# A decoder layer: x for the sums loaded one item sooner on the weight queue, both fifth products of a group in one item, and more steps ahead of two heads' transposes

## The chip, the cores and the metric

The kernel runs on one core of a Trainium2 chip. The metric is device time in microseconds (us) of one launch, the median of several runs. Names of engines: PE is TensorE (PEld its weight loads), DVE is VectorE, ACT is ScalarE, POOL is GpSimd, SP is the SyncE, which here only issues DMAs. "L505" is line 505 of the kernel before.

## The reference

One layer on x of 512 tokens by 1024 channels, in float32. A combined projection gives the columns of three token mixers and three gates. Cut to what matters here:

```
proj = x @ w_in                       # 1024 x 10752
da:  4 heads of differential attention (two softmax maps, lambda, RMS norm, relative bias)
sb:  8 heads of stick-breaking attention (log-space breaks, strictly causal)
dil: 12 heads of dilated windows, 3 groups (window, dilation) x 4 head slots; the three
     outputs of a head slot are weighed by their softmax denominators
merged = sigmoid(g0) * (o_da @ w_branch_da) + sigmoid(g1) * (o_sb @ w_branch_sb)
       + sigmoid(g2) * (o_dil @ w_branch_dil)
x = layer_norm(alpha * x + merged @ w_out)
x = layer_norm(alpha * x + square(relu(x @ w_up)) @ w_down + sigmoid(x @ w_ple_gate) * (p @ w_ple))
```

## The kernel before

**Products.** Every large product keeps close to float32 accuracy by splitting both operands into a high and a low part: `mm3` issues three matmuls (L89 to L91), high by high, high by low, low by high. A weight chunk of 128 x 1024 is loaded into `raw`, ScalarE casts its high part to `wh` (L263), VectorE subtracts to get `wl` (L265). Six `raw` and five `wh`/`wl` buffers go round, so a cast waits until TensorE has finished with the chunk five back.

**Seven products for eight.** Some of the projections (the pairs of dilated values, the query/key groups, the gates, and later the large layers) are cut into 2 x 2 blocks and computed with seven block products instead of eight. That needs sums of weight blocks and sums of x blocks. The sums of weight blocks are made by DMAs from GpSimd that accumulate in memory (`sum_steps`, L1183), one 512 KB transfer a step. The sums of x blocks are made on chip: `load_xr` (L498) loads x again as eight tiles `xr` of 256 KB, each held back until the last weight split issued so far is done; `mixer_forms` (L682) waits five steps, then subtracts blocks on VectorE (L690, L695, L696, L700) and splits the results into the forms u7, u6, u4, u5 (L292, L293).

**Items.** The work of TensorE is a list of items, run in order by the main loop (from L2134). Per item the loop: evacuates the item before (`ev`); issues splits and loads of weights (`pump`, `fill`); adds `size * rate` of the item to a credit, each whole unit of which issues one sum step; runs one step of everything that is in progress beside the items; and issues the item's matmuls. Items of single projections and of da_v give one more step halfway through their matmuls.

The order of items around the change: single projections, four items of da_v, then 14 items of a pair of values (`value_pair`, L531, at `pair_at`), then two groups of eight items (`group_items`, L354), four single projections, a third group, four single projections, then the first branch product and the gates. A group computes the projections of two query/key pairs (j = 0 and 1) with seven products of 256 columns. Its items are: second product for both j; first product for both; seventh and sixth for j = 0, for j = 1; fifth for j = 0, for j = 1 (`of_five`, L436); third and fourth for j = 0, for j = 1. Each is three matmuls by four blocks: a product of one j is 12 matmuls.

**Steps.** Each attention head is a generator that does its next piece at each step; at most eight accumulator banks' worth of heads are in progress, in a fixed order (stick-breaking first, then dilated heads 0, 1, 2, then the differential ones). A dilated head (`dil_head`, L1948) does: first logits (L1965) with their maxima (L1968) and exponentials (L1974); the other logits (L1981, L1989) and exponentials (L1996), and r, the statistics spread for a matmul (L1999, L2002); two steps later the exchange of statistics between partitions (px, L2007 and L2009) and the scaling of the weights (L2031, L2035); then, once all values are there, two transposes into two banks (L2055) with copies pt, one step later two more (L2064), and one step later the output products (L2073, L2078). Their values come through memory: `keep` (L519) stores the projected values on the weight queue, `values_of` (L523) reads them back per head as dl_vh (L528), also on that queue. Head 0 reads them one step after all values are stored, then waits two more steps ahead of its transposes; heads 1 and 2 wait none there; head 3 one.

**Order on the engines.** Items and steps give each instruction its place in the program's text; the order on each engine is then planned when the program is built, by dependences, that order and the planner's own estimates of time, so an instruction can be put ahead of one that comes earlier in the text. On the chip each engine, and each DMA queue's issuer, runs its list strictly in order. Waits for buffers are part of it: a load waits until the tile's former use has ended.

The step count and places that the change touches are numbers in the main loop: `forms_at` is the item at which `mixer_forms` begins, `DA_TABS` the item at which the bias tables of the differential heads are loaded (they are turned six items later).

Of the kernel before, what the change touches and what calls it, by code (L numbers as in the profile page):

```python
# [57 lines left out]
def trunk(tc, a, out):  # L58
    nc = tc.nc
    es = ExitStack()  # L60
    with es:
# [223 lines left out]
        items = []  # L285
# [14 lines left out]
        xt = a["xT"]  # L300
# [53 lines left out]
        def group_items(gi, pairs):  # L354
# [21 lines left out]
            def add(ps, need, free, run, ev, bank):  # L376
                for p in ps:
                    at = {5: 0, 6: 1, 7: 2, 3: 3}.get(p)
                    cs[p] = [chunk(w[{1: 0, 2: 1, 4: 3}[p]] if at is None else qsum[gi][at], 1024)]
                item([c for p in free for c in cs[p]], lambda b: run(), lambda b: ev(),  # L380
                     need=[c for p in need for c in cs[p]], bank=bank)
                items[-1]["rate"] = 0.6

            def put(j, i, h, ps, s=None):

# [47 lines left out]
                    nc.scalar.copy(b["s"][:, HB], b["x"][:, HC])  # L433
                add(() if j else (7, 6), (7, 6), (7, 6) if j else (), run, ev, lambda: both[j]["x"])

            def of_five(j):  # L436
                def run():
                    prod(j, 5, HB, False, False)

                def ev():  # L440
                    put(j, 1, 1, both[j]["x"][:, HB], both[j]["s"][:, HB])
                add(() if j else (5,), (5,), (5,) if j else (), run, ev, lambda: both[j]["x"])

            def of_three_four(j):
                def run():
# [9 lines left out]

            of_two()
            of_one()
            for f in (of_seven_six, of_five, of_three_four):
                for j in range(2):
                    f(j)  # L460

        def first_item():

# [34 lines left out]
        def load_xr():  # L498

            r = {}  # L500
            for h in range(2):
                for th in range(2):
                    for kp in range(2):
                        t = slot("xr")
                        i = nc.gpsimd.dma_start(t.rearrange("p (k t) -> p k t", k=2),  # L505
                                                xt[:, 4 * h + 2 * kp:4 * h + 2 * kp + 2, 256 * th:256 * th + 256])
                        tc.add_manual_dep(getattr(i, "ins", i), lows[-1].name, mybir.DependencyInfo(
                            mybir.DependencyClass.Sync, mybir.DependencyReason.DATA), reason="not ahead of time")
                        r[h, th, kp] = t
            return [[r[h, th, kp] for kp in range(2)] for h in range(2) for th in range(2)]  # L510
# [171 lines left out]
        def mixer_forms():  # L682

            r11, r12, r21, r22 = load_xr()
            for _ in range(5):
                yield

            with tc.issue_after(st["low"]):
                for kp in range(2):
                    nc.vector.tensor_sub(r22[kp], r22[kp], r12[kp])  # L690
            form(xf, 7, r22)
            yield
            for kp in range(2):
                with tc.issue_after(st["low"]):
                    nc.vector.tensor_sub(r12[kp], r11[kp], r12[kp])  # L695
                nc.vector.scalar_tensor_tensor(r11[kp], r22[kp], -1.0, r11[kp], op0=OP.mult, op1=OP.subtract)  # L696
            form(xf, 6, r11)
            yield
            for kp in range(2):
                nc.vector.scalar_tensor_tensor(r21[kp], r11[kp], -1.0, r21[kp], op0=OP.mult, op1=OP.subtract)  # L700
            form(xf, 4, r21)
            yield
            form(xf, 5, r12)
            yield
# [1243 lines left out]
        def dil_head(hd):  # L1948
# [91 lines left out]
            if hd == 0:  # L2040
                yield
                values = values_of(hd)
            for _ in range({0: 2, 3: 1}.get(hd, 0)):
                yield

            src0 = {}
# [77 lines left out]
                except StopIteration:  # L2124
                    pending.remove(g)

        DA_TABS = pair_at[0] + 22
        sum_steps_ = sum_steps()
        credit = 0.0
        forms_at = pair_at[0] - 5  # L2130
        freed = 0
        prev = None
        for n, it in enumerate(items):
# [196 lines left out]
```

## Time and profile before

| | us |
|---|---|
| median of 3 runs | 1054.31 (1051.61 to 1055.39) |
| the profiled execution's own time | 1055.07 |
| its span, first to last instruction | 1053.4 |
| TensorE busy | 1029.4 |
| VectorE busy | 778.7 |
| ScalarE busy | 615.6 |
| GpSimd busy | 198.3 |
| mean granted TensorE clock | 0.989 |

The span starts and ends with the core's first and last instruction; the execution's own time is 1.67 us longer. Times in the views count from the start of the span. In a row of a timeline stand the start, the duration (of a merged run of instructions, the whole run's), the engine, line and operation, output and inputs, and in brackets the idle time just before and what ended it. In a row of windows stand the window, its length, the busy time of TensorE, its weight loads, VectorE, ScalarE and GpSimd with their instruction counts, the granted clock, the busy share of the DMA engines and GB/s. A row of waits has the total, the number of times and the longest.

### The profile page before, as it was taken

The page shows a single profiled execution, that of the slowest core. Times are in us where ns is not written, and L with a number is a line of the kernel's source. Part 1 is how long each engine was busy: PE and PEld are TensorE (multiplying, and loading weights), DVE is VectorE, ACT ScalarE, POOL GpSimd, SP SyncE. Part 2 cuts the span into 40 slices and gives each one's busy share as a digit, 9 for nine tenths or more (in the row PEclk, how much of TensorE's full clock was granted, in tenths as well). Part 3 has the DMA queues.
Part 4 walks back from the last instruction along what each step waited for, and adds up shares of the span by engine and source line. Part 5 has one row for each costly group of instructions (what it writes and reads, how often), then busy time and mean ns, then how long its engine had stood idle before and what let it go on. Part 6 is the DMA issues. An engine that isn't in the chain of part 4 may idle for free.

```text
span 1053.4 us, 15640 instructions
## 1 busy us (share of the span) xinstructions
PE 1029.4 (98%) x5650; PEld 889.5 (84%) x5650; DVE 778.7 (74%) x1387; ACT 615.6 (58%) x1057; POOL 198.3 (19%) x299
## 2 busy tenths in 40 slices
PE   9999999899889999999999999999999999999996
PEld 7888888778779898888888888888999899899885
DVE  6888567577645777667879885888678777777975
ACT  7575466365334566565775753685656566566651
POOL 0314421211102122121301122121212112111001
PEclk9999999899989999999999999999999999999998
DMA  8999997559968969787899999379999999998622
GB/s 305 290 277 290 252 305 258 160 135 270 298 223 257 305 227 276 168 233 215 240 299 258 298 294 306 76 198 325 344 328 323 325 326 331 306 319 270 214 76 80
DMA packets 83629, 270.74 MB, mean 257 GB/s; under 512 B 9720, under 2 KB 16648, under 8 KB 83552
## 3 DMA queue, kind: packets, MB, share of 16 engines
q0 software_dynamic: 35984, 128.79, 48.6%
q1 hardware_dynamic: 46992, 140.04, 36.4%
q8 instruction: 44, 0.72, 0.3%
q10 hardware_dynamic: 576, 0.92, 0.2%
q14 instruction: 33, 0.27, 0.1%
HBM read 262.35 MB, written 112.22 MB: 356 GB/s over the span
## 4 chain that ended last, share of the span: by engine, by line
PE 67%; DVE 2%; ACT 0%; issue 0%; DVEq 0%
PE mm L89 6%; PE mm L90 6%; PE mm L91 6%; PE at L1401 4%; PE at L1402 4%; PE at L1403 4%; PE at L721 3%; PE at L723 3%; PE at L722 3%; PE at L89 2%; PE at L90 2%; PE at L91 2%; PE at L1014 1%; PE at L1013 1%; PE at L1012 1%; PE at L1140 1%
## 5 line engine op out<-in xcount | busy, mean ns | idle before, releaser
L265 DVE TENSOR_TENSOR wl<-raw,wh 128x1024 fp32r<-128x1024 f32 x268 | 323.2, 1214 | 130.6 <-ACT wh L263 129.1
L263 ACT CAST wh<-raw 128x1024 fp32r<-128x1024 f32 x268 | 278.0, 1043 | 218.8 <-PE mm L90 112.7
L89 PE MATMUL mm<-xhT,wh 128*128 128x512 f32 (+1 forms) x254 | 95.5, 376 | 0.0
L91 PE MATMUL mm<-xhT,wl 128*128 128x512 f32 (+1 forms) x254 | 94.2, 371 | 0.0
L90 PE MATMUL mm<-xlT,wh 128*128 128x512 f32 (+1 forms) x254 | 94.2, 371 | 0.0
L1401 PE MATMUL at<-wh,hh 128*128 128x512 f32 x188 | 73.7, 392 | 0.0
L1402 PE MATMUL at<-wl,hh 128*128 128x512 f32 x188 | 73.7, 392 | 0.0
L1403 PE MATMUL at<-wh,hl 128*128 128x512 f32 x188 | 73.1, 389 | 0.0
L89 PE MATMUL mm<-x1hT,wh 128*128 128x256 f32 x256 | 72.8, 284 | 0.0
L90 PE MATMUL mm<-x1lT,wh 128*128 128x256 f32 x256 | 72.4, 283 | 0.0
L91 PE MATMUL mm<-x1hT,wl 128*128 128x256 f32 x256 | 72.4, 283 | 0.0
L91 PEld LDWEIGHTS mm<-xhT,wl 128*128 128x128 f32 x254 | 47.8, 188 | 8.2
L89 PEld LDWEIGHTS mm<-xhT,wh 128*128 128x128 f32 x254 | 47.9, 189 | 7.7 <-PE mm L590 0.2
L90 PEld LDWEIGHTS mm<-xlT,wh 128*128 128x128 f32 x254 | 47.9, 189 | 7.5
L89 PEld LDWEIGHTS mm<-x1hT,wh 128*128 128x128 f32 x256 | 48.9, 191 | 1.9
L90 PEld LDWEIGHTS mm<-x1lT,wh 128*128 128x128 f32 x256 | 48.9, 191 | 1.5
L91 PEld LDWEIGHTS mm<-x1hT,wl 128*128 128x128 f32 x256 | 48.9, 191 | 0.0
L1218 POOL DMA_DIRECT2D usum<-in_wu_dram x32 | 29.8, 942 | 93.9 <-DMA usum<-usum 30.7
L1218 POOL DMA_DIRECT2D dsum<-in_wd_dram x28 | 24.4, 870 | 117.6 <-DVE wl L265 38.1
L1403 PEld LDWEIGHTS at<-wh,hl 128*128 128x128 f32 x188 | 35.3, 188 | 7.7
L1401 PEld LDWEIGHTS at<-wh,hh 128*128 128x128 f32 x188 | 35.5, 189 | 6.2
L1402 PEld LDWEIGHTS at<-wl,hh 128*128 128x128 f32 x188 | 35.5, 189 | 5.7
(672 smaller groups left out, 2863.7 us busy)
## 6 DMA issues: line engine op xcount, KB each, us to landing
usum<-in_wu_dram POOLq DMA_DIRECT2D x48, 512.0 KB, 8.9
dsum<-in_wd_dram POOLq DMA_DIRECT2D x42, 512.0 KB, 8.7
raw<-usum SPq DMA_DIRECT2D x32, 512.0 KB, 8.3
raw<-dsum SPq DMA_DIRECT2D x28, 512.0 KB, 8.4
raw<-in_wt_dram SPq DMA_DIRECT2D x26, 512.0 KB, 6.8
raw<-in_wd_dram SPq DMA_DIRECT2D x25, 512.0 KB, 6.2
raw<-in_wu_dram SPq DMA_DIRECT2D x24, 512.0 KB, 8.1
raw<-in_wv_dram SPq DMA_DIRECT2D x18, 512.0 KB, 6.9
```

Of the source, the lines that this page charges most:

```text
L89: nc.tensor.matmul(ps, wh, xh, start=start, stop=False, skip_group_check=True)
L90: nc.tensor.matmul(ps, wh, xl, start=False, stop=False, skip_group_check=True)
L91: nc.tensor.matmul(ps, wl, xh, start=False, stop=stop, skip_group_check=True)
L263: i = nc.scalar.copy(h, raw)
L265: i = nc.vector.tensor_sub(lo, raw, h.bitcast(F32))
L721: nc.tensor.matmul(ps, h[:, q], c["h"][:, n], start=go, stop=False, skip_group_check=True)
L722: nc.tensor.matmul(ps, h[:, q], c["l"][:, n], start=False, stop=False, skip_group_check=True)
L723: nc.tensor.matmul(ps, lo[:, q], c["h"][:, n], start=False, stop=end, skip_group_check=True)
L1218: i = nc.gpsimd.dma_start(o, i, accum_op=OP.add, max_dma_last_dim=4096)
L1401: nc.tensor.matmul(ps, h[:, q], c["h"][:, s], start=go, stop=False, skip_group_check=True)
L1402: nc.tensor.matmul(ps, h[:, q], c["l"][:, s], start=False, stop=False, skip_group_check=True)
L1403: nc.tensor.matmul(ps, lo[:, q], c["h"][:, s], start=False, stop=end, skip_group_check=True)
```

## The change

In each group both fifth products become one item, so a group has seven items instead of eight, and the credit of a group's item goes from 0.6 to 0.85. The eight loads of xr are issued by SP instead of GpSimd; `mixer_forms` begins one item sooner and waits six steps instead of five. Head 0 waits four steps instead of two ahead of its transposes, and head 1 one instead of none. The bias tables are loaded two item numbers sooner.

```
-                items[-1]["rate"] = 0.6
+                items[-1]["rate"] = 0.85
...
-            def of_five(j):
+            def of_five():
                 def run():
-                    prod(j, 5, HB, False, False)
+                    for j in range(2):
+                        prod(j, 5, HB, False, False)
+                        if not j:
+                            put(0, 1, 1, both[0]["x"][:, HB], both[0]["s"][:, HB])
 
                 def ev():
-                    put(j, 1, 1, both[j]["x"][:, HB], both[j]["s"][:, HB])
-                add(() if j else (5,), (5,), (5,) if j else (), run, ev, lambda: both[j]["x"])
+                    put(1, 1, 1, both[1]["x"][:, HB], both[1]["s"][:, HB])
+                add((5,), (5,), (5,), run, ev, lambda: None)
...
-            for f in (of_seven_six, of_five, of_three_four):
-                for j in range(2):
-                    f(j)
+            for j in range(2):
+                of_seven_six(j)
+            of_five()
+            for j in range(2):
+                of_three_four(j)
...
-                        i = nc.gpsimd.dma_start(t.rearrange("p (k t) -> p k t", k=2),
-                                                xt[:, 4 * h + 2 * kp:4 * h + 2 * kp + 2, 256 * th:256 * th + 256])
+                        i = nc.sync.dma_start(t.rearrange("p (k t) -> p k t", k=2),
+                                              xt[:, 4 * h + 2 * kp:4 * h + 2 * kp + 2, 256 * th:256 * th + 256])
...
             r11, r12, r21, r22 = load_xr()
-            for _ in range(5):
+            for _ in range(6):
                 yield
...
-            for _ in range({0: 2, 3: 1}.get(hd, 0)):
+            for _ in range({0: 4, 1: 1, 3: 1}.get(hd, 0)):
                 yield
...
-        DA_TABS = pair_at[0] + 22
+        DA_TABS = pair_at[0] + 20
         sum_steps_ = sum_steps()
         credit = 0.0
-        forms_at = pair_at[0] - 5
+        forms_at = pair_at[0] - 6
```

## The prediction

> **What bounds the kernel now.** I read the page first, then TensorE's waits over the whole span, then the windows around the slices in which its clock digit falls below 9, and last the timelines of the engines in those windows.
>
> ```profile
> span 1053.4 us, 15640 instructions
> PE 1029.4 (98%) x5650; PEld 889.5 (84%) x5650; DVE 778.7 (74%) x1387; ACT 615.6 (58%) x1057; POOL 198.3 (19%) x299
> ```
>
> ```profile
> PE at L2073 <- DMA dl_vh<-values: 4.3, 1, 4.3
> PE at L2007 <- DVE r L1999: 3.1, 1, 3.1
> PE at L1823 <- DVE spl L1798: 2.6, 1, 2.6
> ...
> PE mm L89 <- DVE dl_q L394: 0.9, 1, 0.9
> PE mm L556 <- DVE da_v L603: 0.9, 1, 0.9
> ...
> PE at L2078 <- DVE pt L100: 0.2, 1, 0.2
> ```
>
> TensorE is busy 98% of the span, so only two things can shorten it: less matrix work, or fewer of the 24 us in which it stands still (1053.4 - 1029.4) and of the time in which it runs at less than the full clock. The change takes away no matrix work. Three waits are long, one each, and all of them lie between 200 and 308 us. The next view gives the busy time of TensorE, VectorE, ScalarE and GpSimd in windows of 4 us, then the granted clock and the DMA share. It shows that each wait costs more than itself.
>
> ```profile
> 200.00:204.00 4.00, 1.82 (x9) 1.16 (x7) 1.54 (x3) 2.24 (x5) 0.00 (x0) 1.00 0.93 189
> 204.00:208.00 4.00, 2.91 (x7) 2.25 (x8) 4.00 (x9) 0.00 (x0) 0.00 (x0) 0.57 0.04 9
> 208.00:212.00 4.00, 4.00 (x12) 3.03 (x12) 3.96 (x8) 0.51 (x1) 0.00 (x0) 0.58 0.00 0
> ```
>
> ```profile
> 280.00:284.00 4.00, 3.33 (x27) 2.89 (x25) 1.30 (x2) 1.54 (x3) 0.61 (x1) 1.00 1.06 287
> 284.00:288.00 4.00, 1.02 (x5) 1.02 (x6) 2.49 (x11) 3.44 (x11) 0.75 (x2) 0.81 1.06 394
> 288.00:292.00 4.00, 4.00 (x20) 3.59 (x19) 3.04 (x14) 2.55 (x9) 0.00 (x0) 0.50 1.02 281
> 292.00:296.00 4.00, 4.00 (x31) 4.00 (x31) 1.26 (x9) 1.15 (x4) 0.00 (x0) 0.84 0.32 97
> 296.00:300.00 4.00, 3.59 (x30) 3.20 (x28) 3.90 (x13) 2.84 (x5) 0.00 (x0) 1.00 0.76 247
> 300.00:304.00 4.00, 0.14 (x1) 0.18 (x2) 1.78 (x3) 0.00 (x0) 0.53 (x1) 0.94 1.02 322
> 304.00:308.00 4.00, 4.00 (x18) 3.44 (x19) 0.00 (x0) 0.00 (x0) 0.00 (x0) 0.63 0.90 351
> ...
> 328.00:332.00 4.00, 4.00 (x35) 4.00 (x35) 0.69 (x1) 1.28 (x3) 2.03 (x3) 1.00 0.93 298
> ```
>
> I price a stall as its idle time plus, for the busy time after it, one minus the granted clock. **Stall one**, at 201.8: idle 2.18 + 1.09 = 3.3, slow 2.91 x 0.43 + 4.00 x 0.42 = 2.9, together 6.2 us. **Stall two**, at 283.8: idle 0.67 + 2.98 = 3.65, slow 1.02 x 0.19 + 4.00 x 0.50 + 4.00 x 0.16 = 2.85, together 6.5 us. **Stall three**, at 299.6: idle 0.41 + 3.86 = 4.3, slow 4.00 x 0.37 = 1.5, together 5.75 us. The sum is 18.4 us of 1053.4.
>
> Only the clock's part of these prices is open to doubt. [...] The trace decides for 6.2: 0.57 and 0.58 follow that wait.
>
> **Stall one, and x on the other queue, one item sooner.** The rows are VectorE's, then GpSimd's, then the weight queue's.
>
> ```profile
> 182.28 1.22 DVE L265 TENSOR_TENSOR wl<-raw,wh 128x1024 fp32r<-128x1024 f32 x1 [0.17 <-ACT wh L263]
> ...
> 197.40 0.69 DVE L1794 SCALAR_TENSOR_TENSOR e<-at,e 128x512 f32<-128x512 f32 x1 [0.60 <-ACT e L1793]
> 202.46 1.35 DVE L690 TENSOR_TENSOR xr<-xr,xr 128x512 f32<-128x512 f32 x2 [4.37 <-DMA xr<-in_xT_dram]
> 203.73 0.69 DVE L1798 TENSOR_TENSOR spl<-e,sph 128x512 fp32r<-128x512 f32 x1
> ```
>
> ```profile
> 189.79 5.34 POOL L505 DMA_DIRECT2D xr<-in_xT_dram  x7
> 198.02 0.72 POOL L505 DMA_DIRECT2D xr<-in_xT_dram  x1 [2.88 <-issue]
> ```
>
> ```profile
> 183.53 5.76 SPq L215 DMA_DIRECT2D raw<-vsum  x2
> 227.70 2.67 SPq L215 DMA_DIRECT2D raw<-in_wv_dram  x2
> ```
>
> The 8 loads of xr leave GpSimd from 189.79 to 198.02, the last alone after 2.88 us. The first subtraction (L690) needs the last pairs, stands ahead of spl in VectorE's order, and holds it from 198.1 to 203.7. TensorE needs spl at 201.8. After the change the same gate, the last split ahead of the loads, is one item older: 182.28 + 1.22 = 183.5 instead of 189. For the issue on the weight queue there is no row of this shape. The nearest are 0.33 us for a weight load and 1.73 / 3 = 0.58 us for a strided read (both below), so 8 x 0.33 = 2.6 to 8 x 0.58 = 4.6 us, done by 186.1 to 188.1. I take the upper one, since xr is strided too. What queues behind them is one load of raw<-vsum (the second of that row, which ends at 189.29), then nothing until 227.70: in this stretch the queue has 38 us to spare, and the weights pay nothing.
>
> ```profile
> DMA to landing us min/median/max: 5.1/8.4/8.5
> ```
>
> These are xr's own landing times today. With the longest of them the last load lands at 188.1 + 8.5 = 196.6. VectorE asks for it at 198.1 today. The forms now wait six steps from a start two half items earlier, so they come one step, half an item, sooner: an item lasts 189 - 183.5 = 5.5 us here, so VectorE might ask 2.7 us sooner, at about 195.4, and lose 1.2 us to it. That still lets spl end by 201.8. I take the whole 6.2 us. The bounds are 0 (x no earlier in effect) and 6.2 plus the 0.9 us of a later wait for VectorE (da_v, in the second fence). Freed GpSimd time (5.34 + 0.72) is worth nothing: it stands idle 81% of the span.
>
> [...]
>
> **Stall three, and the steps ahead of the transposes.** For head 0 the path ends in the read of values back from memory.
>
> ```profile
> SPq L528 <- DMA values<-dl_v: 14.4, 3, 7.2
> ```
>
> ```profile
> 297.24 1.73 SPq L528 DMA_DIRECT2D dl_vh<-values  x3
> 299.88 0.34 SPq L215 DMA_DIRECT2D raw<-in_wq_dram  x1
> ```
>
> ```profile
> 303.86 3.26 PE L2073 MATMUL at<-pt,dl_vh 128*128 128x256 f32 x8 [4.26 <-DMA dl_vh<-values]
> 306.95 1.95 PE L2078 MATMUL at<-pt,dl_vh 128*128 128x128 f32 x16
> 308.74 1.04 PE L2064 MATMUL at<-ident,L 128*128 128x128 f32 x8
> ```
>
> The read is issued no later or sooner than now; only its use moves. Before, the products of head 0 stand ahead of the second fifth product. With two more steps, and both fifth products in one item, they stand behind that product and both items of the third and fourth: 12 + 24 + 24 = 60 matmuls. At 4.00 / 35 = 0.114 us each (the window at 328) that is 6.9 us of other work against a wait of 4.26. More sums come with the higher rate: 7 x 0.85 = 5.95 instead of 8 x 0.6 = 4.8 steps in a group, 1.15 transfers of 512 KB. Read and written at the 287 GB/s of the window at 280, one takes 3.7 us at most, and in the worst case all of it stands ahead of the read: 4.26 + 3.7 = 8.0 leaves 1.1 us of wait. The best case is nothing. I take 5.75 us as gained, with bounds of 0 and 5.75.
>
> **Stall two stays, and grows.** Nothing in the change is aimed at it, and two of its fillers are moved away.
>
> ```profile
> 283.79 1.04 ACT L263 CAST wh<-raw 128x1024 fp32r<-128x1024 f32 x1 [1.66 <-PE at L90]
> 284.74 0.40 ACT L1974 ACTIVATE L<-L,nm 128x128 f32<-128x128 f32 x1
> ```
>
> ```profile
> 280.71 0.93 PE L2055 MATMUL at<-ident,L 128*128 128x128 f32 x7
> ...
> 286.98 0.64 PE L2007 MATMUL at<-r,fold 128*128 128x32 f32 x2 [3.12 <-DVE r L1999]
> 287.43 2.05 PE L2064 MATMUL at<-ident,L 128*128 128x128 f32 x8
> 289.25 0.58 PE L89 MATMUL mm<-u7h,wh 128*128 128x256 f32 x1
> ```
>
> ScalarE's exponentials for head 1 (L1974) stand behind a cast that waits for TensorE to finish a product of the group; r, and so L2007, waits for them. L2055 and L2064 are head 0's transposes. They run inside this stall now. Two steps later they no longer fill it, and cost their own time elsewhere: 0.93 + 1.04 (the full-clock row above) = 2.0 us, unless the program's order puts something else there (0). I take 2.0.
>
> **The rest.** The fifth products as one item are the same 24 matmuls in the same order; three steps and three items fewer remain, and the later work that a step drives runs under a TensorE whose longest wait after 310 is 0.9 us (dl_q). The tables for the later heads move from the second group's first item to the first group's last, and are turned in the same item as before, since one item is gone. Head 1's extra step is paid by the same 60 matmuls. All of these I cost at 0; without that cover, a step's wait like that at L2007 is 6.5 us.
>
> **Sum**, against the profiled execution's own 1055.07: 1055.07 - 6.2 - 5.75 + 2.0 = 1045.1. That execution is 0.76 above the median of 1054.31, so the forecast is **1044**.
>
> **Rivals.** *Stall two goes as well (0.17).* With the transposes gone, the order on VectorE and ScalarE around it is another one, and the casts may fall behind the exponentials. For it: the chain is one of order, not of work. Against it: no line of it is edited. 1054.3 - 6.2 - 5.75 - 6.5 = 1036.
>
> *One of the two stalls stays (0.17).* If xr waits on the weight queue for its tiles to come free, as the 2.88 us ahead of the eighth load may have been, it lands as late as now: 1044.4 + 6.2 = 1050.6. If head 0's products are put forward again ahead of the third and fourth products, stall three stays: 1050.1. *Neither goes (0.08):* 1054.3 to 1056.3.
>
> *Slower (0.10): the two heads in lockstep.* Now head 0 is one step ahead of head 1. With 4 and 1 steps both reach their transposes at the same step: four banks in one step, four in the next, then two outputs and the next group's bank, out of six. The copies that empty them are in VectorE's and ScalarE's order behind casts that wait for TensorE, as at 283.79. One such stall costs 6.5. Two give 1044.4 + 13 = 1057.4, no change; from three on (1063.9) the kernel is slower. Against it: four transposes' banks in one step occur already where head 0's second pair meets head 1's first, with no wait for a copy above 0.2 us.
>
> **How the numbers follow.** The forecast has 0.48, at 1044. A measurement of this kernel can tell about 0.5% from no change, that is 1049 and below, or 1059.6 and above. Forecast and first rival lie below: 0.65 faster. One or neither stall gone lies between: 0.25. Lockstep is left: 0.10. The range goes from the first rival to the case with one stall left and a little beyond, 1036 to 1053, and leaves out the last two. The likeliest case's own range, by its bounds (0.9 less, 2.0 less, 1.1 more plus part of its clock), is 1041 to 1047.
>
> **What would show it.** Right: no wait of TensorE at L1823 and L2073, no wait of L690 for a DMA, the clock at 1.00 where da_v's products begin, xr's loads on the weight queue ahead of 190, and a stall of 3 us or more still ahead of L2007 or of the first u7h product, with low clock behind it. Wrong: VectorE waiting for xr with spl behind it, dl_vh still the releaser of a TensorE wait, or new waits for pt copies in the first two groups.

## The result, and the profile after

The changed kernel takes 1044.65 us (median of 8 runs, 1042.14 to 1047.3), the kernel before beside it 1052.6 (8 runs, 1049.54 to 1055.91). The ratio is 0.9919, with a 95% interval of 0.9897 to 0.9941: faster by 0.8%. The forecast was 1044. The total came out as forecast, but two of its terms were wrong, and the larger part of their errors cancels.

The page after, its first line and the line of busy times:

```profile
span 1043.2 us, 15645 instructions
PE 1025.9 (98%) x5650; PEld 887.6 (85%) x5650; DVE 777.9 (75%) x1387; ACT 614.5 (59%) x1057; POOL 192.3 (18%) x291
```

TensorE's waits after (total, times, longest). The changed kernel's line numbers are five above the old ones from L505 on, so L2012 is the old L2007, L2078 the old L2073, L1828 the old L1823.

```profile
PE at L2012 <- DVE r L2004: 3.1, 1, 3.1
PE mm L817 <- ACT b L823: 2.2, 1, 2.2
PE mm L89 <- DVE dl_q L394: 1.5, 2, 0.9
PE at L89 <- ACT gs L401: 1.3, 1, 1.3
...
PE mm L561 <- DVE da_v L608: 0.3, 1, 0.3
PE at L2083 <- DVE pt L100: 0.2, 1, 0.2
```

The waits for spl (2.6) and for dl_vh (4.3) are gone. The wait for r is there to the tenth. One is new: TensorE waits 2.2 us for ScalarE's copy b of the first branch product.

**Where the time went.** The same product of TensorE, found by line, tiles and count, starts at these times, first in the kernel before, then after: the last product ahead of the first group, one in the first item of the third group, one in the gates, and the last of all.

```profile
272.88 0.39 PE L558 MATMUL at<-wh,xlT 128*128 128x512 f32 x1
375.44 0.28 PE L90 MATMUL at<-xlT,wh 128*128 128x256 f32 x1
520.20 0.39 PE L722 MATMUL at<-wl,xhT 128*128 128x512 f32 x1
1044.80 0.28 PE L1521 MATMUL at<-wh,hl 128*128 128x256 f32 x1
```

```profile
264.63 0.39 PE L563 MATMUL at<-wh,xlT 128*128 128x512 f32 x1
362.79 0.28 PE L90 MATMUL at<-xlT,wh 128*128 128x256 f32 x1
511.16 0.39 PE L727 MATMUL at<-wl,xhT 128*128 128x512 f32 x1
1035.82 0.28 PE L1526 MATMUL at<-wh,hl 128*128 128x256 f32 x1
```

The differences are -8.25, -12.65, -9.04 and -8.98. A product at 183.03 in the kernel before, ahead of stall one, differs by -0.25. So three stretches tell the story, and every run below is read by them: **stretch I** (183 to 273, stall one) -8.00, **stretch II** (273 to 375, stalls two and three) -4.40, **stretch III** (375 to 520) +3.61; nothing moves after. The span is 10.2 us shorter, but the last 1.2 us of that lies after the last store has landed (1050.94 before, 1041.97 after), where no work is left.

**Stall one is gone.** VectorE's subtraction L695 (old L690) runs at 197.40 and waits for nothing. The tile view of xr says how the loads went: SP issues all eight from 183.7 on, and the slowest lands after 6.7 us. The windows show TensorE full and the clock at 1.00 where 0.57 stood.

```profile
197.40 0.69 DVE L695 TENSOR_TENSOR xr<-xr,xr 128x512 f32<-128x512 f32 x1
```

```profile
L510 SPq DMA_DIRECT2D xr<-in_xT_dram x8: 387/420/726, 183.7 to 187.3; - x8
...
DMA to landing us min/median/max: 3.9/6.0/6.7
```

```profile
200.00:204.00 4.00, 4.00 (x21) 3.28 (x21) 4.00 (x8) 0.77 (x2) 0.00 (x0) 1.00 0.42 84
204.00:208.00 4.00, 4.00 (x19) 3.28 (x19) 3.86 (x9) 3.23 (x6) 0.27 (x1) 1.00 0.00 0
```

**Stall two is as it was, stall three is gone.** Windows of the same stretch, 8 us sooner than before: TensorE idle and the clock at 0.50, and then a full window at 300, where TensorE was busy 0.14 us of 4.

```profile
276.00:280.00 4.00, 1.26 (x9) 1.24 (x9) 2.73 (x15) 2.72 (x10) 0.53 (x1) 0.92 1.08 329
280.00:284.00 4.00, 3.37 (x16) 3.00 (x15) 1.74 (x10) 2.08 (x8) 0.00 (x0) 0.50 1.02 372
...
300.00:304.00 4.00, 4.00 (x32) 3.84 (x31) 2.87 (x3) 1.94 (x3) 0.81 (x2) 1.00 1.03 421
```

**Stall four is new.** First the two rows of the timeline (in brackets the idle time and what ended it), then the windows.

```profile
449.17 1.07 ACT L823 COPY b<-mm 128x512 f32<-128x512 f32 x2 [6.79 <-DMA oT<-oT]
...
449.81 0.62 PE L817 MATMUL mm<-wh,oTh 128*128 128x512 f32 x1 [2.20 <-ACT b L823]
```

```profile
444.00:448.00 4.00, 3.61 (x16) 2.63 (x14) 1.18 (x6) 0.00 (x0) 0.00 (x0) 1.00 1.06 244
448.00:452.00 4.00, 2.19 (x6) 1.72 (x7) 1.44 (x9) 2.27 (x6) 0.00 (x0) 0.75 0.70 205
452.00:456.00 4.00, 4.00 (x19) 3.33 (x18) 2.67 (x6) 3.40 (x7) 0.00 (x0) 0.82 0.06 10
```

ScalarE's copy empties TensorE's accumulator bank into a tile. Activations of this kind share one set of 52 tiles, and this one was last used by the fourth dilated head (head 3), whose output `put_away` (L663) stores to memory. The copy waits for that store: ScalarE stands idle for 6.79 us ahead of it. (In the traces of both kernels the program's 5506 matmuls on TensorE, its 1371 instructions on VectorE and SP's 295 and 303 issues start in the order of the built program.) By the prediction's own rule the stall costs 0.39 + 1.81 idle, and 2.19 x 0.25 + 4.00 x 0.18 = 1.3 for the slow clock: 3.5 us, against 3.61 measured in stretch III. The tile view of oT shows what is late, before and then after:

```profile
L658 POOL DMA_DIRECT2D oT<-oT x1: 588/588/588, 448.6 to 448.6; - x1
...
DMA to landing us min/median/max: 3.0/3.0/3.0
```

```profile
L663 POOL DMA_DIRECT2D oT<-oT x1: 599/599/599, 438.6 to 438.6; - x1
...
DMA to landing us min/median/max: 10.4/10.4/10.4
```

The store goes out 10 us sooner, like everything, but takes 10.4 us to land instead of 3.0. GpSimd's timeline has two accumulating transfers of the sums (L1223) and a weight load right ahead of it, and two more sums behind; SP's queue issues a second weight load at 436.21. In the kernel before, both weight loads go out 2.9 and 4.0 us behind the store, at 451.52 and 452.62.

```profile
434.75 0.89 POOL L178 DMA_DIRECT2D raw<-in_wgm_dram  x1 [2.35 <-DVE wl L265]
435.32 1.20 POOL L1223 DMA_DIRECT2D dsum<-in_wd_dram  x1
436.48 0.87 POOL L1223 DMA_DIRECT2D usum<-in_wu_dram  x1
438.63 0.60 POOL L663 DMA_DIRECT2D oT<-oT  x1 [1.27 <-ACT oT L2086]
```

Three groups have 21 items now, at a credit of 0.85: 17.85 sum steps, against 24 x 0.6 = 14.4 before. By the first branch the sums are 3.45 steps ahead, so others of them stand around the store.

### The profile page after: what moved, and what is told of

It reads as the page before. It is cut to its first block, busy times and chain, and to the rows that moved or that the text cites. A ratio compares the mean times of both kernels' runs of the same rounds, so it can differ in the third digit from the quotient of the medians.

```text
span 1043.2 us, 15645 instructions
## 1 busy us (share of the span) xinstructions
PE 1025.9 (98%) x5650; PEld 887.6 (85%) x5650; DVE 777.9 (75%) x1387; ACT 614.5 (59%) x1057; POOL 192.3 (18%) x291
## 4 chain that ended last, share of the span: by engine, by line
PE 95%; DVE 2%; DMA 1%; ACT 1%; issue 1%; DVEq 0%; ACTq 0%
PE mm L89 10%; PE mm L90 10%; PE mm L91 10%; PE at L1406 4%; PE at L1407 4%; PE at L1408 4%; PE at L726 3%; PE at L727 3%; PE at L728 3%; PE mm L595 2%; PE mm L593 2%; PE mm L594 2%; PE at L89 2%; PE at L90 2%; PE at L91 2%; PE at L1017 1%
## 5 line engine op out<-in xcount | busy, mean ns | idle before, releaser
L1223 POOL DMA_DIRECT2D usum<-in_wu_dram x32 | 28.4, 898 | 94.4 <-DVE wl L265 40.7
L1223 POOL DMA_DIRECT2D dsum<-in_wd_dram x28 | 23.3, 833 | 117.0 <-DVE wl L265 46.8
```

The source lines that it names most:

```text
L1223: i = nc.gpsimd.dma_start(o, i, accum_op=OP.add, max_dma_last_dim=4096)
```

## The experiments

Two questions were open: whether the gains are separate and which half of each edit makes them, and what stall four is. All runs are in the table: time, ratio to the kernel before with its interval, and how far TensorE moved in each stretch against the kernel before.

| kernel | us | ratio (95%) | I | II | III |
|---|---|---|---|---|---|
| the change | 1044.65 | 0.9919 (0.9897 to 0.9941) | -8.00 | -4.40 | +3.61 |
| x alone | 1045.58 | 0.9922 (0.9905 to 0.9939) | -7.96 | -0.40 | -0.01 |
| steps alone | 1048.97 | 0.9959 (0.9944 to 0.9973) | -0.61 | -5.19 | -0.01 |
| x, queue only | 1052.22 | 0.9981 (0.9966 to 0.9995) | -2.66 | -2.19 | -0.03 |
| x, one item sooner only | 1046.89 | 0.9935 (0.9919 to 0.9952) | -7.99 | -0.20 | -0.03 |
| change, sums' rate kept | 1040.91 | 0.9886 (0.9869 to 0.9904) | -7.99 | -5.19 | -0.58 |
| merged item alone | 1058.23 | 1.0059 (1.0040 to 1.0079) | -1.66 | +0.52 | +3.59 |
| change, head 1 later | 1046.74 | 0.9939 (0.9916 to 0.9961) | -7.96 | -2.21 | +3.88 |
| change, store on SP | 1046.27 | 0.9936 (0.9921 to 0.9951) | -7.96 | -4.97 | +2.37 |
| x and steps, no merged item | 1040.46 | 0.9861 (0.9847 to 0.9876) | -8.00 | -6.50 | -0.04 |
| change, rate kept, head 1 later, more steps | 1037.01 | 0.9828 (0.9812 to 0.9845) | -7.98 | -7.94 | -0.53 |
| change, rate lower | 1045.79 | 0.9908 (0.9889 to 0.9927) | -7.98 | -4.70 | +5.76 |
| x, head 1 later, more steps, no merged item | 1037.88 | 0.9852 (0.9823 to 0.9882) | -8.01 | -8.00 | -0.01 |

The stretches repeat far better than the times. The time also holds what happens ahead of 183 us, where executions differ by up to 4.5 us (last section). A stretch that still has a stall in it repeats less well: the clock behind a wait at the same place falls in some executions and not in others, which is worth up to 2.9 us (0.57 at stall one in the kernel before, 1.00 in "x, queue only"; 0.75 at stall four in the change, 1.00 in "store on SP").

### x alone

```
-                        i = nc.gpsimd.dma_start(t.rearrange("p (k t) -> p k t", k=2),
+                        i = nc.sync.dma_start(t.rearrange("p (k t) -> p k t", k=2),
...
-            for _ in range(5):
+            for _ in range(6):
...
-        forms_at = pair_at[0] - 5
+        forms_at = pair_at[0] - 6
```

> The kernel before with the x loads alone changed: on the queue of the weights and one item sooner; the fifth products, their rate, the tables and the steps are as before. My theory (three separate stalls, whose prices add): stall one alone goes. No wait of TensorE at the sums' subtraction, VectorE's subtraction shows no DMA as its releaser, the granted clock is 1.00 through 184 to 208, and the fixed products of group 0 start 6.2 to 8.25 us sooner than before (8.25 is what the changed kernel shows there). Stall three (TensorE waiting for dl_vh at the first dilated head's products, 4.26 us in the kernel before) stays, since the steps aren't there; head 3's store doesn't collide with the sums, since their rate is the old one. Span 6 to 8.5 us under the kernel before, time about 1046 to 1048. Rival (the gain of the change comes from the steps, and the sums' wait is covered by something else): under 2 us.

Measured: stretch I -7.96, as with the whole change; II and III stand still, with TensorE waiting 3.8 us for dl_vh. Stall one is this edit's, all of it, and has nothing to do with the others. The edit alone is worth as much as the whole change (0.9922 against 0.9919): what the rest of the change gains in stretch II it loses again in stretch III.

### Steps alone

```
-            for _ in range({0: 2, 3: 1}.get(hd, 0)):
+            for _ in range({0: 4, 1: 1, 3: 1}.get(hd, 0)):
```

> The kernel before with the steps alone: four instead of two ahead of the first dilated head's transposes and one ahead of the second's. My theory: stall three alone goes (no wait of TensorE for dl_vh), stall one stays with its 2.65 us wait and its slow clock, stall two stays. Span 4 to 6 us under the kernel before; time 1048.5 to 1050.5. Rival A (the new wait for head 3's stored output at 447 in the changed kernel comes from the shifted steps and not from the rate of the sums): TensorE waits some 2 us behind the ScalarE copy of the first branch here too, and the gain is 2.5 us or less. Rival B (without the higher rate of the sums there is not work enough in the two steps to cover the load): part of the dl_vh wait is left.

Measured: -5.19 in stretch II, nothing in III, and no wait behind the first branch's copy, so rival A falls: the steps don't make stall four. No wait for dl_vh is left either, so the higher rate was not needed as cover (rival B falls).

### x, queue only

```
-                        i = nc.gpsimd.dma_start(t.rearrange("p (k t) -> p k t", k=2),
+                        i = nc.sync.dma_start(t.rearrange("p (k t) -> p k t", k=2),
```

> The kernel before with the x loads on the queue of the weights and nothing else, so they are issued at the same item as before. Theory: what makes the data late in the kernel before is the time that GpSimd takes to issue (eight loads in 8.2 us, the last in 2.9); SyncE issued the same eight in 3.6 us in the changed kernel. The last lands about 198 to 200 instead of 203.8, and the wait of TensorE is under 1 us: at least 4 of the 6.2 us are gained by the queue alone. Rival (a queue is only a place to issue from, and the time of the issue decides): the landing moves by under 1 us and the stall stays at 2 to 3 us with its slow clock; gain under 1.5 us.

Measured, by the tile view of xr in this kernel:

```profile
L505 SPq DMA_DIRECT2D xr<-in_xT_dram x8: 408/472/962, 192.6 to 197.2; - x8
...
DMA to landing us min/median/max: 4.3/7.4/7.8
```

The last one lands at 204.6, not at 198 to 200 (203.1 in the kernel before), and TensorE waits 1.9 us at the sums (1.2 for sph, 0.7 for spl). This execution was 3.28 us late by 183 us; counted from there, the last landing is 1.7 us sooner than before. SP issues faster (0.47 us a load in the median, 1.04 from GpSimd before), but the issue starts at the same split and the transfers take 7.4 us in the median and 7.8 at most (8.4 and 8.5 before). My expectation fell and its rival comes nearer. Yet stretch I shows -2.66. The idle time from 200 to 212 is 2.9 us, against 3.3 before, so that is 0.4 of it. Most of the rest is the clock, which stays at 1.00 here, where 0.57 and 0.58 cost the kernel before 2.9 us:

```profile
208.00:212.00 4.00, 3.00 (x13) 2.48 (x14) 4.00 (x9) 1.50 (x4) 0.00 (x0) 1.00 0.00 0
```

With the x loads untouched the clock fell, to 0.50 behind a wait of 1.8 us (steps alone, stretch I -0.61) and to 0.66 behind one of 1.7 (merged item alone, -1.66). That the other queue kept it up is not shown. The -2.19 in stretch II is no gain of the edit: a TensorE that comes later waits less for dl_vh (2.7 us here, 4.3 before).

### x, one item sooner only

```
-            for _ in range(5):
+            for _ in range(6):
...
-        forms_at = pair_at[0] - 5
+        forms_at = pair_at[0] - 6
```

> The kernel before with the x loads one item sooner, still issued by GpSimd. Theory: the issue starts about 6 us sooner and takes 8.2 us again, so the last lands about 197 to 198, ahead of the subtraction at 197.4 in the changed kernel or at most 1 us behind it: the stall goes as well or leaves under 1 us, and the span gains 5 to 8 us. Either half of the edit would then have been enough. Rival (GpSimd's issue is held by its sums, and starting sooner lets the sums' own transfers get between): the last lands after 200 and a wait of 1 us or more with a slow clock stays; gain under 4 us.

Measured, the tile view of xr again, now from GpSimd:

```profile
L505 POOL DMA_DIRECT2D xr<-in_xT_dram x8: 708/712/737, 183.9 to 188.9; - x8
...
DMA to landing us min/median/max: 4.2/5.5/7.2
```

The last lands at 196.06, ahead of the subtraction at 197.5, and stretch I is -7.99: the whole of stall one, with the queue unchanged. **The earlier item was the edit; the other queue adds nothing to it.** The gap of 2.88 us ahead of the eighth load is gone too, although GpSimd still issues.

### The change with the sums' rate kept

```
-                items[-1]["rate"] = 0.85
+                items[-1]["rate"] = 0.6857
```

> The changed kernel with one number different: a group's item gives the sums a credit of 0.6857 instead of 0.85, so that seven items give the 4.8 steps that eight items of 0.6 gave before, and the sums stand where they stood. My theory on the new wait (TensorE 2.2 us behind ScalarE's copy of the first branch at 447.6 us, 3.65 us with the slow clock behind it): head 3's store lands 10.4 us after its issue because the sums, 3.45 steps ahead (21 items of 0.85 against 24 of 0.6), send three transfers just ahead of it and two behind. Here the store lands in 3 to 5 us, the wait is gone, and TensorE is 3 to 4 us ahead of the changed kernel from there on; stalls one and three stay away. Span about 1039.5 to 1040.5, time about 1041. Rival A (the wait comes from the shifted steps and the merged item, not from the sums): the wait and the 3.65 us stay. Rival B (the higher rate was needed as cover for the load of dl_vh): 1 to 4 us of the dl_vh wait come back at 300 us.

Measured: stretch III -0.58, no wait behind the first branch's copy, 1040.91 us. Rivals A and B fall: without the extra sums the wait is gone, and no dl_vh wait comes back. The store lands after 7.2 us, later than I expected, but that is soon enough. In GpSimd's timeline stand now a load and two plain copies of the sums (L1225) ahead of it:

```profile
433.96 0.88 POOL L178 DMA_DIRECT2D raw<-in_wgm_dram  x1 [2.62 <-DVE wl L265]
434.53 0.86 POOL L1225 DMA_DIRECT2D dsum<-dsum  x1
435.06 0.85 POOL L1225 DMA_DIRECT2D usum<-usum  x1
437.85 0.57 POOL L663 DMA_DIRECT2D oT<-oT  x1 [1.93 <-ACT oT L2086]
```

So the higher rate is not all of it. Of the 7.4 us by which the store's landing time grew (3.0 to 10.4), 4.2 are there with the old number of sums (3.0 to 7.2). In all seven kernels with the merged item the two weight loads and two or more sums go out close ahead of the store; in all seven without it only one copy does. TensorE waits only where those sums are accumulations.

### The merged item alone

```
-                items[-1]["rate"] = 0.6
+                items[-1]["rate"] = 0.85
...
+            of_five()
...
-        DA_TABS = pair_at[0] + 22
+        DA_TABS = pair_at[0] + 20
```

> The kernel before with the merged fifth item, the credit of 0.85 and the earlier tables alone; the x loads and the steps are as before. Theory: no gain by itself, stalls one, two and three stay (together some 18 us of idle time and slow clock); the store of head 3 collides with the sums as in the changed kernel, and TensorE loses about 3.5 us at 456 to 460. Time 0 to 4 us over the kernel before. Rival A (the merged item and the sums' rate carry part of the gain, by fewer waits in the group or more work over the load of dl_vh): 1 us or more faster than before. Rival B (the collision needs all the parts together): within 1 us of before, and no wait behind the first branch's copy.

Measured: slower by 0.6%, and +3.59 in stretch III with the same wait (2.3 us at L817, the store landing after 10.5 us). The theory holds; the median is 5.4 us above that of the kernel before, where 0 to 4 were expected, but the profiled execution is only 2.2 us behind at its last product. By itself this part of the change only makes stall four.

### The change with the store on SP

```
-            nc.gpsimd.dma_start(kept_oT[k], oT.pop(k), max_dma_last_dim=4096)
+            (nc.sync if k == 11 else nc.gpsimd).dma_start(kept_oT[k], oT.pop(k), max_dma_last_dim=4096)
```

> The changed kernel with only head 3's store of its output issued by SyncE instead of GpSimd; the sums stay as they are. Theory A (the store is late because it stands behind the sums' transfers in GpSimd's queue): it lands in 3 to 5 us, the wait behind the first branch's copy at 447 us is gone, and TensorE is 3 to 4 us ahead of the changed kernel after it. Theory B (the store is late because the DMA engines as a whole are busy with the sums and the weights, whichever queue it is in): it lands after 7 us or more again, and the wait stays at 1 to 2.5 us.

```profile
L663 SPq DMA_DIRECT2D oT<-oT x1: 319/319/319, 441.9 to 441.9; - x1
...
DMA to landing us min/median/max: 11.2/11.2/11.2
```

On a queue without sums the store lands after 11.2 us and TensorE waits 2.7 us: theory B. With no sums in its queue the store is no sooner than behind them (10.4 us), so its place in GpSimd's queue is not what makes it late. What is left is the traffic around it, an inference: no run changes that alone. (The comparison is not quite clean: two sums that stood behind the store on GpSimd now go out 1.4 and 0.8 us ahead of it.) The x loads got little from another queue alone, too: 7.4 us from issue to landing in the median, against 8.4.

TensorE waits longer than in the changed kernel (2.7 us against 2.2), but stretch III loses less (+2.37 against +3.61), because the clock does not fall here:

```profile
452.00:456.00 4.00, 2.17 (x9) 1.80 (x10) 0.96 (x7) 2.75 (x7) 0.00 (x0) 1.00 0.66 197
456.00:460.00 4.00, 4.00 (x22) 3.37 (x21) 3.77 (x7) 3.42 (x7) 0.00 (x0) 1.00 0.24 79
```

### The change with a lower rate

```
-                items[-1]["rate"] = 0.85
+                items[-1]["rate"] = 0.5
```

> The changed kernel with the sums' credit at 0.5 instead of 0.85, so the sums stand 3.9 steps behind those of the kernel before by the first branch. It asks whether the rate itself or only where the sums stand at 432 to 440 us makes head 3's store late. Theory (what counts is how many sum transfers are issued close around the store, and the first branch issues them at its own rate of 2.4): the store lands in 5 to 8 us, as with the rate kept, and lighter traffic in the groups lets dl_vh land up to 2 us sooner, without moving TensorE; time within 1.5 us of 1040.9. Rival A (sums that are late are missed later): waits for sums of 1 us or more in the gates or after, and a time over 1043. Rival B (the rate alone makes the store late): it lands in 3 us and the time is 1 us or more under 1040.

Measured: the store lands after 11.6 us, TensorE waits 3.4 us at L817, stretch III loses 5.76. A lower rate doesn't cure stall four, so it isn't the height of the rate. Ahead of the store stands what stood there in the changed kernel, accumulations and the load:

```profile
431.59 1.11 POOL L1223 DMA_DIRECT2D dsum<-in_wd_dram  x1
434.24 0.89 POOL L178 DMA_DIRECT2D raw<-in_wgm_dram  x1 [1.53 <-DVE wl L265]
434.79 2.01 POOL L1223 DMA_DIRECT2D usum<-in_wu_dram  x2
438.12 0.60 POOL L663 DMA_DIRECT2D oT<-oT  x1 [1.31 <-ACT oT L2086]
```

The theory and both rivals missed. The rate is a phase: it decides which sums fall ahead of the store. With two or more accumulations and a load just ahead, the store took 10.4, 10.5, 10.8, 11.2 and 11.6 us in five kernels; with a load and two copies 7.2 and 7.5 in two; with one copy, issued some 2 us ahead of it, and both weight loads behind, 2.9 to 3.1 in the seven without the merged item (the kernel before among them). That accumulations are what weighs, and not the count or the distance, these rows suggest; no run isolates it. The lighter traffic did bring dl_vh sooner: its last load lands at 290.4 instead of 298.1, which moves nothing, since nobody waits for it any more.

### x and steps, without the merged item

The two edits of x alone and steps alone together; a group keeps eight items, 0.6 and the old tables.

> The kernel before with the x loads changed (weight queue, one item sooner) and the steps changed, and nothing else: the fifth products stay two items with a credit of 0.6 and the tables stay where they were. Theory (stalls one and three are separate and their gains add; the merged item brings nothing of its own): TensorE stands 8.0 (as with the x loads alone) plus 5.2 us (as with the steps alone) = 13.2 us ahead of before from 320 us on and keeps it, with no wait behind the first branch's copy; span about 1040, time about 1041, within 1 us of the changed kernel with the sums' rate kept. Rival A (the two overlap, since work that comes sooner meets the same DMA landing of dl_vh): part of the dl_vh wait comes back and the gain is 10 us or less. Rival B (the merged item is worth something by itself): it is 2 us or more behind the kernel with the merged item and the kept rate.

Measured: 1040.46 us, -8.00, -6.50 and -0.04. The gains add and rival A falls. Stretch II is even 1.3 us better than the -5.19 of the steps alone, but by the clock: it stands at 0.60 in one window behind the wait for r and at 1.00 in the next, where the steps alone have 0.68, 0.50 and 0.97 (1.6 against 2.8 us by the prediction's price, with the idle time the same within 0.1). The merged item shows no worth here: the kernel with it and the kept rate is 0.8 us behind over the three stretches (-13.76 against -14.54), and the clock behind the wait for r makes 1.0 of difference there too (2.6 against 1.6 us).

### The change with head 1 begun later

```
+            if hd == 1:
+                yield
...
-            for _ in range({0: 4, 1: 1, 3: 1}.get(hd, 0)):
+            for _ in range({0: 4, 3: 1}.get(hd, 0)):
```

(The yield stands ahead of the head's first logits.)

> The changed kernel with the second dilated head begun one step later, and its extra step ahead of the transposes taken away, so its end stays where it was. It aims at stall two (TensorE waits 3.1 us for r of head 1, 1.3 for the gate's scale, 0.6 for the evacuation dl_q, and runs at 0.50 to 0.73 of the clock for some 6 us after): VectorE's r and the other logits now stand behind the evacuations dl_q, and ScalarE's exponentials behind the gate's scale. Theory (stall two is an order of work on VectorE and ScalarE: the head's statistics stand ahead of the evacuation that TensorE's next product needs): the wait at the exchange falls under 1 us, the clock stays 1.00, and the group gains 5 to 7 us against the changed kernel. Rival (the chain logits, exponentials, r has its own length and the wait only moves one step on): TensorE waits 2 us or more for r or for the pt copies later, gain under 2 us.

Measured, TensorE's waits between 268 and 330:

```profile
PE mm L89 <- DVE dl_q L394: 3.9, 1, 3.9
PE at L2085 <- DMA dl_vh<-values: 2.9, 1, 2.9
```

Half the theory and half the rival. The wait for r is gone, and the first u7h product starts at 277.76 instead of 281.00. But VectorE's evacuation dl_q (277.29) still comes after a weight split, which waits for its cast, and head 1's first logits, so 3.9 us of one wait are left in place of three waits with 5.0. Then the gain was lost: TensorE reached head 0's products sooner, dl_vh landed later (its last load at 302.8), and stall three was back. Stretch II is 2.2 us worse than with the change.

### Rate kept, head 1 later, more steps

Head 1 as above, the rate 0.6857, and:

```
-            for _ in range({0: 4, 1: 1, 3: 1}.get(hd, 0)):
+            for _ in range({0: 6, 1: 2, 3: 1}.get(hd, 0)):
```

> The changed kernel with the sums' credit at 0.6857, the second dilated head begun one step later, and two more steps again: six ahead of the first head's transposes, two ahead of the second's. Theory (the later start takes 3.6 us out of stall two, as it did alone; what it lost was the load of dl_vh, which landed at up to 302.8 us and made TensorE wait 2.9 us for it; two more steps, some 7 us of products, cover that): no wait for dl_vh, TensorE 16 to 17 us ahead of before from 330 us on and no wait at 447; span about 1036, time 1037 to 1038.5. Rival (the transfers set the pace of this stretch, so whatever is taken from one wait comes back in the next): a wait of 2 us or more for dl_vh, for weights or for a pt copy stands between 290 and 330 us, and the time is no better than with the rate kept alone (1040.9).

Measured: 1037.01 us, ratio 0.9828 (0.9812 to 0.9845). It beats both kernels. TensorE is 16.4 us ahead over the stretches; the only wait between 268 and 330 is dl_q's 3.9, and the windows where dl_vh was waited for are full (3.96 and 4.00 us of 4 from 296 to 304).

The theory holds, and the rival (a wait that always comes back) falls: two more steps were cover enough.

### The same without the merged item

x as changed, head 1 begun later and six and two steps, on the kernel before.

> The kernel before with the x loads changed, the second dilated head begun one step later, and six steps ahead of the first head's transposes and two ahead of the second's: what was best so far, without the merged item, its credit and the earlier tables. It asks what the merged item is worth once the stalls are gone. Theory (nothing, or a loss of up to 0.8 us, which is how far the kernel with x and steps alone stood ahead of the one with the merged item and the kept rate by 320 us, both counted from 180 us): TensorE stands 16.5 to 17.5 us ahead of before at the end, head 3's store lands in about 3 us instead of 7.5, and the time is 1036 to 1037.5. Rival (here the merged item makes work long enough to cover the load of dl_vh, which landed at 299.9 us): a wait of 1 us or more for dl_vh or pt at 290 to 310 us, time over 1038.5.

Measured: 1037.88 us, -8.01, -8.00, -0.01. No wait for dl_vh, and the store lands after 2.9 us. TensorE is 16.0 us ahead over the stretches, less than the 16.5 to 17.5 that I gave (the time is 0.4 us over the range I gave too), and 0.4 behind the run above. So with the kept rate the merged item cost 0.8 us in one pair of kernels and brought 0.4 in the other: nothing that these runs can tell from none.

## Why the prediction was right, and where it was not

- **Stall one: right, and undersized.** It was predicted gained whole at 6.2 us. Stretch I shows 8.00: 7.2 by 229 us, and 0.8 more at the da_v products, whose wait fell from 0.9 to 0.3. The prediction had that wait as a possible loss. The last x load landed at 193.96, ahead of the 196.6 reckoned, and VectorE asked at 197.40, not at 195.4. The remaining 1 us is in the price: idle time plus one minus the granted clock understates this stall, though it fits stall four (3.5 against 3.61); why is open.
- **The clock after short waits: right in the two profiles, but not always so.** In the kernel before, 0.57 and 0.58 follow stall one (3.3 us idle). Stall four waits 2.2 us, and 0.75 and 0.82 follow it. With the store on SP the same product waits 2.7 us, and 1.00 follows. At stall one the clock fell to 0.66 and 0.50 behind waits of 1.7 and 1.8 us and stayed at 1.00 behind 1.9 us in two pieces. So 2.9 of the 6.2 us were a price that the profiled execution paid and another might not; what decides is not shown.
- **Which half carries it: the earlier item.** The prediction reckons one landing time for both halves together. The item alone gives all 8 us (-7.99); the queue alone leaves 1.9 us of the wait.
- **Stall three: right.** The loads of dl_vh for head 0 land by 298.1, and the product that waited starts at 300.93, 2.8 us later. The prediction had 6.9 us of cover against 4.26, which is 2.6 to spare. The worst case (3.7 us for the added sums ahead of the read) didn't occur: with the kept rate the last of these loads lands at 296.1, 2.0 us sooner.
- **Stall two stays: right. The 2.0 us for its lost fillers: too much.** The planner put the seven transposes of L2060 into the stall, which the prediction had named as its bound of 0; TensorE's other waits there grew by 0.76 (gs, 0.54 to 1.30) and 0.63 (dl_q). Stall three's 5.75 less these 1.4 is 4.35, and stretch II shows 4.40. With the kept rate or with the steps alone the dl_q wait isn't there and 5.2 are left, so the term is 0.6 to 1.4. Where the clock recovered sooner (x and steps, -6.50) nothing of it is seen.
- **"The rest" at nothing: wrong.** The step that failed weighed the higher rate at one place, ahead of the read of dl_vh, and said of everything later that TensorE's longest wait after 310 was 0.9 us. But the credit adds up over three groups, and 3.45 steps of sums move against the rest of the program. The merged item itself, put at nothing as "the same 24 matmuls in the same order", also goes with two weight loads ahead of head 3's store that were behind it. At 438 us the store meets these transfers, takes 7.4 us longer to land, and holds a tile that ScalarE needs: +3.61 us. The merged item with its credit makes it without the other edits, the kept rate takes it away.
- **The sum.** Predicted: -6.2, then -5.75 + 2.0 = -3.75, then 0, together -9.95. Measured: -8.00, -4.40, +3.61, together -8.8. What was undersized early (2.45) paid for most of what was missed late (3.61). That is luck, and so is how close the level came: the forecast went from a median of 1054.31 and so was a gain of 10.3 us, while the kernel before took 1052.6 beside the change, so the medians show a gain of 8.0.
- **The rivals.** "Stall two goes as well" did not happen; with head 1 begun one step later (and the load of dl_vh covered) stretch II goes from -5.19 to -7.94 with the merged item and from -6.50 to -8.00 without it, so the order around it is worth 1.5 to 2.75 of the 6.5 us (0.3 and 1.3 of that by a clock that fell less); the rest stands in the wait for dl_q. "One stall stays" did not happen. "Lockstep" did not either: the longest wait for a pt copy is 0.2 us, and with six and two steps none is seen between 268 and 330.

## What to carry to other kernels

A number that spreads background transfers over the program is a phase, not only a rate: after changing it, look at every store and load whose landing somebody waits for, far behind the edit too, and see which transfers stand ahead of it now (head 3's store took 3.0 us to land before and 10.4 after). Starting a late transfer sooner was worth the whole stall here (-7.99 us in stretch I); moving it to another issuer as well added nothing to that (-7.96), and did not bring a late store sooner (11.2 us against 10.4). Each short wait in these runs cost its idle time, and a slow clock only in some executions (0.75 behind 2.2 us, 1.00 behind 2.7 us), so a comparison of two kernels that both still have the stall needs the clock beside it. And where one landing time bounded a stretch, taking a wait out ahead of it gained nothing until the use of that landing was moved as well (stretch II: -2.21 with head 1 later and the wait for dl_vh back, -7.94 with more steps ahead of that use and the sums' rate kept).

## What was not expected of the hardware

Executions differ early, in a part that no edit touches. At 128 us VectorE reads rv, which goes out to memory and comes back; the two rows are of the kernel before and of the kernel with the x loads on the other queue only.

```profile
127.65 0.43 DVE L1837 CAST ah<-a 128x512 fp32r<-128x512 f32 x1 [2.91 <-DMA rv<-rvs]
```

```profile
129.34 0.43 DVE L1837 CAST ah<-a 128x512 fp32r<-128x512 f32 x1 [5.05 <-DMA rv<-rvs]
```

And the window behind it in the second kernel:

```profile
132.00:136.00 4.00, 4.00 (x13) 3.13 (x12) 3.27 (x7) 1.14 (x3) 1.72 (x4) 0.62 1.07 219
```

In the first the data come just in time. In the second they come about 2 us later, TensorE waits 1.5 us for ah, and the clock falls to 0.62: 3.7 us in all (TensorE goes from 0.43 ahead of the kernel before to 3.28 behind it). Five of the twelve experiments lose 0.6 to 4.2 us there. It is a fifth stall that is there in some executions only. The kernel before ran between 1049.54 and 1058.74 us, and this stall is not the whole reason: its profiled execution doesn't have it and took 1055.07. Of this kernel's runs beside the experiments, those below 1050.7 us had a mean granted clock of 0.993 to 0.995, those above 1055 one of 0.988 to 0.991. So the clock behind the stalls, this one or the others, is likely a large part of the spread; no run separates them.
